# Queries, keys, gates and merge gates as 25 block-product pairs in one stage, and the dilated attention beside the branch products

## The chip, the cores and the metric

The kernel runs on one core of one Trainium2 chip. Five engines work side by side, each with an instruction queue that it executes in order: TensorE (PE in the profile, with its weight loads as PEld), VectorE (DVE), ScalarE (ACT), GpSimd (POOL) and SyncE (SP, which here issues most of the DMAs). They meet through semaphores. The metric is the time of one execution in microseconds (us), as the median of three runs. The profile shows one more execution, taken by the hardware profiler.

## The reference

One encoder block on 1024 tokens of width 1024 (`h` is the normalised input):

```python
h = rms_norm(x, g_pre)
a_qkv, bq, bk, bv, mq, ga, gb, gm, mg = split(h @ w_in)      # 1024 x 10496 in all
# A: 3 groups of 8 heads of 64, dilation 1, 4, 16, window of +-64 steps
aq, ak = rope(a_q, pos), rope(a_k, pos)
for g in groups: outs[g], lses[g] = dilated_window_attention(aq[g], ak[g], av[g])
oa = sum_g softmax_g(lses)[g] * outs[g]
# B: grouped-query attention with normalised queries and keys and axial rope; M: attention into 256 memory rows
ya = (oa * silu(ga)) @ w_br_a;  yb = (ob * silu(gb)) @ w_br_b;  ym = (om * silu(gm)) @ w_br_m
gates = sigmoid(mg + b_merge)                                 # 3 x 1024 columns: 24 units of 128
out = (gates[0]*ya + gates[1]*yb + gates[2]*ym) @ w_out
return x + rms_norm(out, g_post)
```

The projection `h @ w_in` is the largest part. Group A alone has 12 units of 128 columns for queries, 12 for keys and 12 for values; the SiLU gates have 12 units, the merge gates 24.

## The kernel before, in words

All operands are fp32. A matrix product is made from three passes: each operand is split by `split` (lines 104 to 106) into a rounded high part (ACT) and a remainder (DVE), and TensorE adds high x high, high x low and low x high. The tokens `h`, transposed, lie split in `hh[0..7]` and `hl[0..7]`, eight tiles of 128 x 1024 each.

There are two ways to make a unit, which is 128 columns of the projection for all 1024 tokens:

- *Plain* (`dense`, lines 139 to 147): 8 row blocks x 3 passes x 2 halves of 512 tokens = 48 matmuls with 512 columns. A unit can be cut anywhere, so `weave` (line 176) deals its matmuls out between the pieces of an attention: it compares the share of the filling that is done with the share of the attention that is done, by costs that the program gives each piece, and takes the one that is behind. Small jobs of the filling (evacuations, splits) stand in `pend` and are emitted one per three matmuls.
- *Pair* (Strassen's scheme in Winograd's form, `PRODUCTS`, line 896): two units by two token halves, each with two halves of the inner dimension, as seven block products instead of eight. A product has 4 row blocks x 3 passes = 12 matmuls, a pair 84. The sums of weight blocks (S1 to S4) are made on POOL, split by ACT and DVE, and the sums of token blocks (T1 to T4) are made once, kept in DRAM (`tsd`) and fetched and split where needed. Partial results are added on DVE as products leave PSUM.

The order of the stages, with the start of each in the profiled execution where the prediction speaks of it:

1. Norm, the keys and values of B, memory keys and values, queries of B and M, attention M; filling: plain gate units.
2. Attention B (`b_att`, from 218 us); filling (lines 868 to 877): five plain SiLU gate units and two plain merge gate units (`FILL_B`).
3. Values of A as block products (462 and 539 us).
4. Keys of A (579 us, lines 1251 to 1292): six pairs. Each result is multiplied by the rotation's cosine and sine tables (`turn_it`) and both products are stored to DRAM (`kd`).
5. Dilated attention (694 us, `item`, `plan`, lines 1399 to 1656): twelve items, one per head pair `p_` and group `g`, eight score tiles of 128 queries each. Per tile: scores (L1467, L1474, written into four PSUM banks `s1`, two tiles to a pair of banks), minimum with mask on DVE (L1486), exponential on ACT (L1487), transposes (L1498, L1513, L1522) three tiles later, a copy to SBUF on ACT (L1500, L1525), value products (L1539, L1546). `scores(1)` is emitted behind tile 3 and the next item's `scores(0)` behind tile 7, each behind value products. The filling is 16 plain units: the twelve query units of A, rotated in the same stage (DVE L1330, L1333, POOL L1334), and four SiLU gates (`GATES_A`). Keys come back from DRAM and are added on POOL (L1397).
   When the three groups of a head pair are done, `combine` (from L1658) weighs them: statistics are transposed and stored (L1572 to L1579), fetched (L1671), made into weights (L1676 to L1687), stored (L1692), fetched as broadcasts (L1666), multiplied in on DVE (L1701) and summed on POOL (L1703). The first three head pairs are combined in this stage, the last in the next.
6. Merge gates (982 us, lines 1714 to 1975): eleven pairs; sums of weights L1813, results to sigmoid form (DVE L1842, ACT L1843) and to DRAM (`thd`).
7. Branch products (1192 us, `y_unit`): 24 units of 24 matmuls, each attention output times its gate, split, times the branch weights; DVE multiplies each with its merge gate from `thd` (L2027, L2029) and POOL adds up (L2030).
8. Output product as block products and the last norm (1323 us).

From stage 3 on ACT, DVE, POOL and SP follow the order in which the program emits their work (`manual_schedule`), so what is emitted earlier on an engine runs earlier there, even when it has to wait.

Of the kernel before, what the change touches and what calls it, by code (L numbers as in the profile page):

```python
# [14 lines left out]
D = 1024  # L15
# [35 lines left out]
def block(ctx: ExitStack, tc: tile.TileContext, x, xT, memT, cst, msk, bcst, tabA, gpost,  # L51
# [5 lines left out]
    hp = ctx.enter_context(tc.tile_pool(name="hp", bufs=16))  # L57
# [78 lines left out]
    hh = [hp.tile([P, S], R, name=f"hh{k}", tag="big") for k in range(8)]  # L136
    hl = [hp.tile([P, S], R, name=f"hl{k}", tag="big") for k in range(8)]
# [73 lines left out]
    spilled = set()  # L211

    def add_filler(j):
        spilled.add(j)

        def evac(half, p):
            th = fp["p"].tile([P, 512], F32, name="fth", bufs=2)
            V.tensor_tensor(th, p, rb[:, half * 512:half * 512 + 512], op=OP.mult)
            A.activation(th, th, AF.Tanh, scale=0.5, bias=hbm[:, j:j + 1])
            nc.sync.dma_start(thd[j, :, half * 512:half * 512 + 512], th)  # L220
        add_unit(wu[U_M + j], evac)

# [17 lines left out]
    kd = dram.tile([2, 12, P, S], F32, name="kd")  # L240
# [471 lines left out]
    with tc.tile_pool(name="ba", bufs=1, reuse_waits="tile") as ba:  # L712
# [157 lines left out]
        for i in (2, 1, 0):  # L870
            for p_ in range(4):
                if (i, p_) not in ((2, 0), (2, 1), (2, 2)) + GATES_A:
                    add_gate(i, p_)
                    ng += 1
        for j in FILL_B:
            add_filler(j)
            ng += 1
# [20 lines left out]
    for k, t in enumerate(ready.pop(len(queue))):  # L898
        SB[0, k] = t
    vpp, vp = pool("vp")  # L900
# [24 lines left out]
    def parts_of(t):  # L925
        return t[:, lo], t[:, hi]
# [86 lines left out]
    def v_banks():  # L1013
# [5 lines left out]
    KT_PLACE = {"T2": ["kT20", "kT21", "kT22", "kT23"], "T3": ["vA220", "vA221", "kT32", "kT33"],  # L1019
                "T1": ["vA110", "vA111", "vA210", "vA211"], "T4": ["vS20", "vS21", "vA120", "vA121"]}  # L1020

    def kt_load(nm, k):
        KT[nm, k] = vb.tile([P, 1024], R, name=KT_PLACE[nm][k])
        nc.sync.dma_start(KT[nm, k][:, hi].bitcast(F32), tsd[int(nm[1]) - 1, k])
# [4 lines left out]

    KR = {}  # L1030

    def k_load(n, u):

        KR[n, u] = wp.tile([P, 1024], F32, name="wr", bufs=WR)
        nc.sync.dma_start(KR[n, u], wu[4 * n + 2 * u + 1])


    AU = [2 * m for m in range(12)] + [U_G + 4 * i + p_ for i, p_ in GATES_A]
    AR, AW = {}, {}

    def a_fetch(n):
        AR[n] = wp.tile([P, 1024], F32, name="wr", bufs=WR)
        nc.sync.dma_start(AR[n], wu[AU[n]])

# [1308 lines left out]
```

## Time and profile before

| | us |
|---|---|
| median of 3 runs | 1409.36 (1407.35 to 1410.84) |
| the profiled execution | 1409.89 |
| its span | 1408.1 |
| TensorE busy / DVE / ACT / POOL | 1384.0 / 1051.2 / 655.7 / 501.9 |
| keys, 579 to 694 | 115.1 |
| dilated attention, 694 to 982 | 287.8 |
| merge gates, 982 to 1192 | 210.1 |
| branch products, 1192 to 1323 | 131.1 |

An engine is busy while one of its instructions executes; TensorE's matmuls are pipelined, so the durations of neighbours overlap, and the spacing of their starts tells how fast they go. In a row of grouped instructions stand the line, the engine, the operation, output and input tiles, the shape and the count, then the busy time of the group, the mean duration of one in ns, and the idle time of the engine before them with what ended it. A row of the timeline starts with the start and the duration in us.

### The profile page before, as it was taken

To read this page: it belongs to the slowest core of one execution; us is meant where nothing else is said; L and a number is where in the kernel's file an instruction comes from. 1 tells how busy PE (TensorE), PEld (TensorE's weight loads), DVE (VectorE), ACT (ScalarE), POOL (GpSimd) and SP (SyncE) were. 2 spreads that over 40 slices of the span, in tenths; PEclk is the share of its full clock that TensorE was granted. 3 is DMA by queue.
4 is the path that set the end of the run, shared out by engine and by line. 5 is a ranking of instruction groups with operands and counts; after the bars stand their busy time and mean duration, and the time that the engine had idled before them with its cause. 6 is when DMAs were issued, how large, how long until landed. Compare 5 with 4: busy or idle time off the path is not lost.

```text
span 1408.1 us, 22008 instructions
## 1 busy us (share of the span) xinstructions
PE 1384.0 (98%) x7864; PEld 1120.3 (80%) x7864; DVE 1051.2 (75%) x1839; ACT 655.7 (47%) x1398; POOL 501.9 (36%) x390
## 2 busy tenths in 40 slices
PE   7999999999999999999999999999999999999997
PEld 7799986666656789988888878788888888888886
DVE  7768677767764697888775777765878688677977
ACT  6544465666555445222146666656443334222232
POOL 0507702675766000332153353621333331034303
PEclk9999999999999999999999999999999999999999
DMA  6356532322210788345544464455343543865255
GB/s 233 103 180 213 185 109 87 108 90 72 82 56 27 238 258 250 103 167 180 186 132 114 124 170 118 140 149 179 106 149 127 178 173 128 321 218 209 95 204 179
DMA packets 125950, 216.05 MB, mean 153 GB/s; under 512 B 33616, under 2 KB 62096, under 8 KB 125840
## 3 DMA queue, kind: packets, MB, share of 16 engines
q1 hardware_dynamic: 110192, 189.17, 42.0%
q10 hardware_dynamic: 15648, 25.47, 5.0%
q8 instruction: 62, 1.02, 0.3%
q14 instruction: 48, 0.39, 0.1%
HBM read 149.21 MB, written 65.37 MB: 152 GB/s over the span
## 4 chain that ended last, share of the span: by engine, by line
PE 86%; DVE 4%; ACT 4%; DMA 2%; POOL 2%; issue 2%; SPq 1%; DVEq 0%; ACTq 0%; POOLq 0%
PE s L125 24%; PE sc L125 9%; PE d L143 6%; PE d L147 6%; PE d L145 6%; PE s L1177 4%; PE s L2125 4%; PE ov L809 3%; PE s L1226 3%; PE s L794 2%; PE s L793 2%; PE tr L775 2%; PE d L2125 2%; PE s L1474 2%; PE tr L1546 1%
## 5 line engine op out<-in xcount | busy, mean ns | idle before, releaser
L143 PE MATMUL d<-hh,wh 128*128 128x512 f32 x480 | 194.3, 405 | 2.5 <-DVE fth L228 2.5
L145 PE MATMUL d<-hl,wh 128*128 128x512 f32 x480 | 193.4, 403 | 0.0
L147 PE MATMUL d<-hh,wl 128*128 128x512 f32 x480 | 190.3, 396 | 0.0
L800 POOL TENSOR_TENSOR bl<-bl,bp 128x512 f32<-128x512 f32 x96 | 130.8, 1363 | 54.4 <-ACT bp L796 49.0
L105 ACT ACTIVATE wh<-wr 128x512 fp32r<-128x512 f32 (+1 forms) x93 | 72.2, 787 | 124.5 <-PE sc L125 75.1
L106 DVE TENSOR_TENSOR wl<-wr,wh 128x1024 fp32r<-128x1024 f32 (+1 forms) x67 | 85.6, 1289 | 52.1 <-ACT wh L105 52.0
L125 PE MATMUL sc<-hh,wh 128*128 128x512 f32 x384 | 118.7, 390 | 0.0
L143 PEld LDWEIGHTS d<-hh,wh 128*128 128x128 f32 x480 | 90.3, 188 | 28.0 <-issue 5.5
L147 PEld LDWEIGHTS d<-hh,wl 128*128 128x128 f32 x480 | 90.5, 189 | 21.2 <-issue 4.7
L1487 ACT ACTIVATE pra<-pra,sts 128x192 f32<-128x192 f32 (+2 forms) x192 | 80.9, 423 | 54.3 <-DVE sts L1486 54.1
L145 PEld LDWEIGHTS d<-hl,wh 128*128 128x128 f32 x480 | 90.5, 189 | 19.5 <-issue 4.7
L796 ACT ACTIVATE bp<-s 128x512 f32<-128x512 f32 x128 | 75.7, 595 | 43.3 <-PE s L794 42.2
L776 DVE TENSOR_REDUCE bn<-tr 128x1 f32<-128x512 f32 x128 | 84.8, 683 | 12.3 <-PE tr L775 11.3
L125 PEld LDWEIGHTS sc<-hh,wh 128*128 128x128 f32 x384 | 72.0, 188 | 15.7 <-DVE wh L106 0.4
L1330 DVE SCALAR_TENSOR_TENSOR t2a<-d,tab 32x512 f32<-32x512 f32 x96 | 66.0, 687 | 22.0 <-PE d L147 18.6
L2030 POOL TENSOR_TENSOR acc<-acc,th 128x1024 f32<-128x1024 f32 x15 | 41.3, 2756 | 107.9 <-DVE th L2029 107.9
L1813 POOL TENSOR_TENSOR sf<-wr 128x512 f32<-128x512 f32 x22 | 30.8, 1422 | 131.4 <-DVE ch L106 45.7
L125 PE MATMUL sc<-hl,wh 128*128 128x512 f32 x192 | 74.7, 389 | 0.0
L125 PE MATMUL s<-hh,ch 128*128 128x512 f32 x224 | 73.7, 390 | 0.0
L1334 POOL TENSOR_TENSOR aq<-t1a,t2a 128x512 f32<-128x512 f32 x24 | 46.9, 1955 | 71.5 <-DVE t1a L1333 71.5
L1843 ACT ACTIVATE rs<-rs,hbm 128x512 f32<-128x512 f32 x44 | 31.8, 722 | 75.5 <-DVE rs L1842 75.5
L1397 POOL TENSOR_TENSOR ak<-kraw,kswp 128x512 f32<-128x512 f32 x24 | 45.9, 1939 | 51.7 <-DMA std<-sr 20.0
(507 smaller groups left out, 3748.7 us busy)
## 6 DMA issues: line engine op xcount, KB each, us to landing
wr<-in_wu SPq DMA_DIRECT2D x64, 512.0 KB
th<-thd SPq DMA_DIRECT2D x24, 512.0 KB
thd<-rs ACTq DMA_DIRECT2D x44, 256.0 KB
kd<-vy ACTq DMA_DIRECT2D x32, 256.0 KB
g2d<-fth SPq DMA_DIRECT2D x24, 256.0 KB
wos<-os SPq DMA_DIRECT2D x12, 512.0 KB
kraw<-kd SPq DMA_DIRECT2D x12, 512.0 KB
kswp<-kd SPq DMA_DIRECT2D x48, 128.0 KB
```

Source lines behind the costliest of these rows:

```text
L105: A.activation(dst_h, src, AF.Copy)
L106: V.tensor_tensor(dst_l, src, dst_h.bitcast(F32), op=OP.subtract)
L125: PE.matmul(out_ps, a, b, start=i == 0, stop=i == n - 1)
L143: PE.matmul(dst, wh[:, k, :], hh[k][:, t], start=k == 0, stop=False)
L145: PE.matmul(dst, wh[:, k, :], hl[k][:, t], start=False, stop=False)
L147: PE.matmul(dst, wl[:, k, :], hh[k][:, t], start=False, stop=k == 7)
L776: fp["last"] = V.tensor_reduce(st[i]["n"][:, j, c:c + 1], s, axis=AX.X, op=OP.min)
L796: A.activation(pp, s, AF.Exp, scale=-1.0)
L800: G.tensor_tensor(lsum[i % 2], lsum[i % 2], pp, op=OP.add)
L1330: V.scalar_tensor_tensor(t2[i], p[j], -0.125, tab[1][j, t], op0=OP.mult, op1=OP.mult)
L1487: A.activation(src, src, AF.Exp, scale=-1.0, bias=bias, accum_out=sts[:, h, 1, T:T + 1])
L2125: PE.matmul(dst[:, e[0]:e[1]], a, b, start=k == 0 and q == 0, stop=k == 3 and q == 2)
```

## The change

- Keys and merge gates, until now two stages of pairs, become one stage of 25 pairs: twelve pairs that make the queries and the keys (`("rope", m)`), one pair of SiLU gates (`GATES_P`) and twelve of merge gates, in alternation (`PAIRS`). Queries are no longer plain units. Two SiLU gates more take the place of the two merge gates beside attention B.
- Products that end in the same sum accumulate in one PSUM bank (`skip_group_check`); ACT copies the intermediate values out (`keep_copy`) where DVE added before. The next pair's first product stands between a pair's own.
- The weights' columns are laid out so that the two units of a query or key pair hold the first and the second half of each head's rotation. `c_fin` multiplies by the tables (DVE), `turn_it` adds (POOL), in the order of the group's classes, and `k_store` writes finished queries and keys to `qkd`.
- The dilated attention stands behind that stage. Its filling is the first 16 of the 24 branch units, in the order memory, B, A (`add_y`); the last eight, branch A, follow. Operands of the memory branch are loaded, multiplied and split in the last pair (`op_load`, `op_mult`, `op_split`). `y_split` makes the remainders of branch weights on POOL there; transposed probabilities are copied on DVE instead of ACT; weighting of the first three head pairs moves from DVE to POOL. The last head pair is combined at the end of this stage (`ending`).
- Sums, evacuations and the output stage keep their arithmetic; some tiles get other places.

```diff
-    for n in range(6):
-        for i, (an, bn) in enumerate(PRODUCTS):
...
+    TURNS = [(j, c, g) for c in range(2) for g in range(3) for j in (1, 0)]
+    pairs = [(8 * i + f, 8 * i + f + 1) for i in (2, 1, 0) for f in range(0, 8, 2)]
+    others = [("gate", 0)] + [("merge", m) for m in range(12)]
+    PAIRS = [x for m in range(12) for x in (("rope", m), others[m])] + [others[12]]
...
+    def c_fin(n, u, t, ps_=None):
+        r = kr() if ps_ is not None else RV.pop((n, u, t))
+        src = r if ps_ is None else ps_
+        kind, m = PAIRS[n]
+        if kind != "rope":
+            V.tensor_tensor(r, src, rb[:, half[t]], op=OP.mult)
...
+                A.activation(r, r, AF.Tanh, scale=0.5, bias=hbm[:, j:j + 1])
+                nc.scalar.dma_start(thd[j, :, half[t]], r)
+            return
...
+    def turn_it(n, t):
...
+        G.tensor_tensor(half_of(o1, t, g), classes(ac, g), classes(bs, g), op=OP.subtract)
+        G.tensor_tensor(half_of(o2, t, g), classes(as_, g), classes(bc, g), op=OP.add)
...
+    def op_load(t):
+        for k in range(4):
+            if k % 2 == 0:
+                OPM[t, k // 2] = vb.tile([P, 1024], F32, name=f"vA12{k // 2}")
+            for dst, src in ((OPM[t, k // 2], od), (tab[k // 2], g2d)):
+                nc.sync.dma_start(dst[:, half[k % 2]], src[2, k, :, t])
...
+    def y_split(m, E=V):
+        if m < len(steps):
+            t = wp.tile([P, 1024], R, name="wh")
+            A.activation(t[:, lo], YW[m][:, lo], AF.Copy)
+            E.tensor_tensor(t[:, hi], YW[m][:, lo], t[:, lo].bitcast(F32), op=OP.subtract)
...
+    def th_load(m):
...
+            THS[m] = wp.tile([P, S], F32, name="wl")
+            nc.sync.dma_start(THS[m], thd[8 * i + f])
+
+    def y_evac(m, t, ps_):
...
+            V.scalar_tensor_tensor(th[:, t], th[:, t], 1.0, ps_, op0=OP.add, op1=OP.mult)
+            (V if m == 23 else G).tensor_tensor(accs[f][:, t], accs[f][:, t], th[:, t], op=OP.add)
...
+    pair_product(0, "A11")
+    pair_product(0, "A12")
+    keep_copy(p1, 0)
+    for n in range(last + 1):
+        N = n + 1
+        pair_product(n, "S2")
+        c_add(*((n - 1, 0, 1, BANK[n - 1, "W"], v_) if n else (0, 0, 0, BANK[0, "Y"], p1)))
+        k_block(n, "A22")
...
+        pair_product(n, "S1")
+        keep_copy(v_, n)
...
+            op_split(lo, 2)
+            op_split(lo, 3)
+            qk_first(0)
+            y_load(0)
+            op_load(hi)
+            y_load(1)
+            qk_first(1)
+        pair_product(n, "S3")
+        k_block(n, "S4")
...
+        pair_product(*((N, "A11") if n < last else (n, "S4")))
+        keep_copy(y_, n)
...
+        pair_product(n, "A22")
...
+        pair_product(N, "A12")
+        c_fin(n, 1, 0, BANK[n, "X"])
+        k_block(N, "S2")
...
+        pair_product(n, "S4")
...
-                A.activation(pp[:, :k], tp[:, :k], AF.Copy)
+                V.tensor_copy(pp[:, :k], tp[:, :k])
...
-                V.tensor_tensor(ogv, ogv, wv, op=OP.mult)
+                (G if p_ < 3 else V).tensor_tensor(ogv, ogv, wv, op=OP.mult)
                 if g:
                     G.tensor_tensor(ogs[0], ogs[0], ogs[g], op=OP.add)
...
+        def add_y(m):
+            n, i, f = steps[m]
+            def gen(_):
+                pend.extend([lambda: th_load(m + 1), lambda: y_load(m + 2), lambda: y_split(m + 1, G)])
+                for t in half:
+                    ps_ = psd()
+                    wh, wl = YW[m]
+                    for k in range(4):
+                        gh, gl = [x[k][:, t] for x in OPER[i]]
+                        for q, (a, b) in enumerate(((wh[:, k], gh), (wh[:, k], gl), (wl[:, k], gh))):
+                            PE.matmul(ps_, a, b, start=k == 0 and q == 0, stop=k == 3 and q == 2)
+                            yield 216
+                    pend.append(lambda t=t, ps_=ps_: y_evac(m, t, ps_))
+            queue.append((lambda: None, gen, 24 * 216.0))
...
+        def ending():
+            com = combine(3, [OG.pop((3, x)) for x in range(3)])
+            return [(com[0], 100.0), (out_pool, 100.0), (lambda: dl_mult(2), 100.0), (lambda: dl_split(2, half), 6000.0),
+                    (com[1], 3000.0), (com[2], 100.0), (lambda: [wo_load("B11", k) for k in range(2)], 100.0),
+                    (com[3], 4000.0), (lambda: [wo_load("B11", k) for k in range(2, 4)], 100.0),
+                    (com[4], 5000.0), (com[5], 100.0), (com[6], 100.0), (com[7], 100.0),
...
+                    (lambda: dl_mult(3), 3000.0), (lambda: dl_split(3, half), 3000.0)] + [
+                    (lambda k=k: wo_split("B11", k), 1500.0) for k in range(4)]
...
+        weave(16, every(), FIRST_PAD + 12 * (NT * (SOFT + 100.0) + 2 * JOINED + 100.0) + 5 * LAST_PAD + 33000.0)
...
-FILL_B = (16, 17)
-GATES_A = ((0, 0), (0, 1), (0, 2), (0, 3))
+FIRST_PAD, LAST_PAD = 7000.0, 1000.0
+GATES_P = ((0, 2), (0, 3))
```

More of the change, by code (lines that the diff above doesn't have):

```diff
@@ L1294, in block @@
+    c_fin(last, 1, 0, BANK[last, "X"])
+    for k in range(4):
+        op_split(hi, k)
+    r = RV[last, 0, 1]
+    V.tensor_tensor(r, BANK[last, "Z"], r, op=OP.add)
+    c_fin(last, 0, 1)
+    c_fin(last, 1, 1)
     close(kpp)
+    close(tbp)
     close(vbp)
```

751 lines of the change are left out of this document (273 added, 478 removed).

## The prediction

> **What bounds the kernel now.** The first view is the page's busy shares.
>
> ```profile
> span 1408.1 us, 22008 instructions
> PE 1384.0 (98%) x7864; PEld 1120.3 (80%) x7864; DVE 1051.2 (75%) x1839; ACT 655.7 (47%) x1398; POOL 501.9 (36%) x390
> ```
>
> TensorE has a matmul in flight for 98% of the span; the others are far below. A busy share is only a hint, so I read the stages next: the chain of waits, which gives their borders, and then the busy time of each engine in each stretch (columns: PE, weight loads, DVE, ACT, POOL, granted clock, DMA share, GB/s).
>
> ```profile
> 579.34 115.13 PE s L125 x504
> 982.23 207.36 PE s L125 x912
> 1189.59 2.72 PE d L125 x12
> 1192.31 131.08 PE sc L125 x576
> ```
>
> ```profile
> 462.08:539.27 77.19, 77.19 (x339) 63.19 (x338) 61.63 (x98) 35.24 (x59) 0.00 (x0) 1.00 0.83 265
> 579.34:694.47 115.13, 115.13 (x505) 94.73 (x505) 96.55 (x125) 27.62 (x46) 34.03 (x21) 1.00 0.48 159
> 694.47:982.23 287.76, 284.90 (x2389) 232.72 (x2388) 204.22 (x598) 166.60 (x546) 107.71 (x55) 1.00 0.53 147
> 982.23:1192.31 210.08, 210.08 (x925) 173.47 (x926) 169.00 (x214) 89.28 (x138) 72.38 (x45) 1.00 0.42 141
> 1192.31:1323.39 131.08, 131.08 (x577) 107.95 (x577) 97.38 (x84) 34.70 (x55) 41.35 (x15) 1.00 0.63 223
> ```
>
> Keys (579 to 694), merge gates (982 to 1192) and branch products (1192 to 1323) run without any gap on TensorE: 504, 924 and 576 matmuls of 512 columns at 228.4, 227.4 and 227.6 ns each. I take 227.7 ns. The dilated attention (694 to 982) has 2.9 us of gaps. Its filling is these three groups, restricted to that stretch:
>
> ```profile
> L143 PE MATMUL d<-hh,wh 128*128 128x512 f32 x256 | 104.9, 410 | 0.0
> L145 PE MATMUL d<-hl,wh 128*128 128x512 f32 x256 | 104.5, 408 | 0.0
> L147 PE MATMUL d<-hh,wl 128*128 128x512 f32 x256 | 100.9, 394 | 0.0
> ```
>
> 768 matmuls, or 174.9 us; so the attention's own matmuls and transposes take 284.9 - 174.9 = 110.0 us of TensorE, and the filling covers everything else. So TensorE's issue time is the bound, and what matters is the number of matmuls and whether TensorE is ever left with nothing.
>
> **The change, part by part.** *Number of matmuls.* A plain unit of 128 columns costs 48 matmuls, a block-product pair (two units) 84. Before: 30 plain units and 17 pairs. After: 14 plain units (7 remain beside the axial attention, as before, two of them now gates instead of merge gates) and 25 pairs. 16 x 48 = 768 go and 8 x 84 = 672 come: 96 fewer, 21.9 us.
>
> *By stage.* Pairs: 25 x 84 = 2100 x 0.2277 = 478.2. Attention: its own 110.0 plus 16 branch units of 24 matmuls, 384 x 0.2277 = 87.4. The eight branch units behind it: 192 x 0.2277 = 43.7. Together 719.4, against 115.13 + 287.76 + 210.08 + 131.08 = 744.0 before. Everything else stays (218.0 and 244.1 to 462, 117.3 for the values, 84.7 at the end). Without any new wait the span would be 1408.1 - 24.6 = 1383.5. What is left is the price of thinner cover: filling per score tile falls from 48/8 to 23/8 matmuls, about 6 to 3.
>
> *Pair stage: costed at nothing.* Per pair DVE does one split of 1024 and thirteen to fourteen operations of 512 (five splits, three sums from PSUM, some six rotations or gate products), 14 x 0.69 + 1.3 = 11.0 us of the pair's 19.1. The key stage did it with 96.55/6 = 16.1 us of DVE per pair and lost nothing. POOL gets the rotation's sums, ACT the tanhs; neither fills a pair. The 96 stores of rotated rows and 50 weight loads queue on SP but are needed a pair or more later. The bounds are 0 and the price of the third rival; I take 0, as the key stage's row is the nearest.
>
> *Entry to the attention.* The first branch unit needs od[2] x gate split into hh and hl, and half of it overwrites tokens that the last product reads. On SP that load stands behind the first queries and keys and a weight: 2 x 0.524 + 0.262 + 8 x 0.262 = 3.4 MB, startable when product S2 of the last pair has let go of its tokens, 2.7 us into the pair. At the 265 GB/s of the values stage (a rate under load, so an estimate) that is 12.9 us, to 15.6. Then come the second gate product, a last merge gate's product and tanh, and four splits one after another.
>
> ```profile
> L1881 DVE SCALAR_TENSOR_TENSOR ot<-ot,raw 128x1024 f32<-128x1024 f32 x2 | 2.4, 1222 | 0.0
> L106 DVE TENSOR_TENSOR wh<-wr,wh 128x512 fp32r<-128x512 f32 x23 | 15.7, 685 | 1.8 <-ACT wh L105 1.8
> L1843 ACT ACTIVATE rs<-rs,hbm 128x512 f32<-128x512 f32 x2 | 1.4, 724 | 2.8 <-DVE rs L1842 2.8
> ```
>
> 15.6 + 1.2 + 0.7 + 0.7 + 0.6 + 4 x 0.7 = 21.6, where TensorE, after 60 matmuls of the shortened last pair (13.7) and 12 + 9 of the first unit (4.8), wants the fourth split at 18.5. That is a wait of 3 us, and 1 more as ACT copies a bank behind two splits in that pair: 4 (0 if the load comes early, 8 if the product waits for the whole).
>
> *Within the attention.* Some 23 filling matmuls per item keep TensorE supplied if DVE and ACT finish in time. DVE loses the rotation and gains ACT's 80 copies of transposed probabilities and 32 branch evacuations:
>
> ```profile
> L1330 DVE SCALAR_TENSOR_TENSOR t2a<-d,tab 32x512 f32<-32x512 f32 x96 | 66.0, 687 | 22.0 <-PE d L147 18.6 <-POOL aq L1334 1.7
> L1487 ACT ACTIVATE pra<-pra,sts 128x192 f32<-128x192 f32 (+2 forms) x192 | 80.9, 423 | 54.3 <-DVE sts L1486 54.1
> L1525 ACT ACTIVATE app<-tr 128x384 f32<-128x384 f32 (+1 forms) x64 | 33.5, 523 | 26.3 <-PE tr L1522 16.3 <-PE tr L1513 9.5
> ```
>
> 66.0 goes from DVE, 80 x 0.52 = 42 of copies (at ACT's price) and 32 x 0.69 = 22 of evacuations come, which is even; but the weight splits and nine weighted products of 2.0 go to POOL, so DVE's 204 us falls to about 160 in a stage of about 212, and ACT's 167 to about 130. Neither is the bound on average. POOL gets sixteen splits of branch weights, those products and sixteen sums; the split for unit 6 stands behind two products and sums of the first head pair, about 6 us, with fifteen filling matmuls and half an item, some 8 us, as cover: nothing, and each microsecond by which POOL is later is TensorE's. Twelve items at a quarter microsecond each make 3 us. Before lost 2.9 (lower bound 0); the upper bound is the second rival.
>
> *End of the attention.* The last head pair's combination stood beside eleven merge pairs; now branch units 16 to 23 need its result. The chain, from an earlier head pair (SP, DVE, POOL):
>
> ```profile
> 843.05 3.10 SPq L1579 DMA_DIRECT2D std<-sr  x3
> 848.05 1.30 SPq L1671 DMA_DIRECT2D cpt<-std  x2
> 858.94 1.25 SPq L1692 DMA_DIRECT2D wgd<-ceg  x2
> 860.84 3.71 SPq L1666 DMA_DIRECT2D wgt<-wgd  x6
> ```
>
> ```profile
> 856.70 0.17 DVE L1676 TENSOR_TENSOR cmn<-cpt 128x16 f32<-128x16 f32 x1
> 858.70 0.21 DVE L1687 TENSOR_TENSOR ceg<-ceg,cds 128x48 f32<-128x48 f32 x1
> 865.83 2.00 DVE L1701 TENSOR_TENSOR og<-og,wgt 128x1024 f32<-128x1024 f32 x1 [1.04 <-DMA wgt<-wgd]
> 868.10 1.96 DVE L1701 TENSOR_TENSOR og<-og,wgt 128x1024 f32<-128x1024 f32 x1 [0.27 <-DMA wgt<-wgd]
> 870.20 2.39 POOL L1703 TENSOR_TENSOR og<-og 128x1024 f32<-128x1024 f32 x1 [4.33 <-DVE og L1701]
> ```
>
> Statistics to SBUF 0.7, four stores and landing 3.0 (846.15 to 848.05 bounds the landing by 1.9), fetch and landing 3.2, weights 2.2, store to the start of the first product 6.9 (858.94 to 865.83), then three products paced by their loads to about 6.5 later, the last POOL sum 2.4, gate product 1.2, first split 1.3: 27.4 us. In the built order 79 branch matmuls follow that last transpose of statistics (18.0 us), with the last value products (1.1) and nine matmuls of unit 16 (2.0): 21.1. In two queues more is waiting. On SP the weight loads stand behind a load of thd that waits for POOL's sum of unit 13; by my count that frees as the chain arrives. On POOL the split of unit 16's weights stands behind the last sums, and TensorE wants it at the unit's third matmul, 1.5 us sooner. So TensorE waits 27.4 + 1 - 21.1 + 1.5 = 8.8, of which I take 8.5; between 3, if loads land faster, and 13.
>
> Sum: 1383.5 + 4 + 3 + 8.5 = 1399.0. The profiled execution took 1409.89 for a span of 1408.1, so 1.8 lies outside it, and it stood 0.5 above the median of 1409.36: 1399.0 + 1.8 - 0.5 = 1400.3, 0.6% faster. A measurement here can tell about 0.3%, 4.2 us.
>
> **Rivals.** *Covers are thicker than I think*: entry and end cost 0 and 3 and items nothing. 1383.5 + 3 + 1.3 = 1388; I round to 1390.
>
> *Slower: the hand-over of score banks.* The third and fourth score tiles of a half item go to banks that the softmax of the third and fourth before must have read; after the value products TensorE waits there.
>
> ```profile
> 856.43 0.35 DVE L1486 CUSTOM_DVE_ANT_0 pra<-s,mask 128x192 f32<-128x192 f32 x1
> 856.01 1.48 PE L1546 MATMUL tr<-app,avs 128*64 128x128 f32 x24
> 857.42 1.81 PE L1474 MATMUL s<-ak,aq 64*128 64x128 f32 x24
> ```
>
> DVE was done at 856.8, the second half of the scores ran from about 858.3: 1.5 us in hand. Three filling matmuls fewer per tile bring TensorE there up to 4 x 3 x 0.228 = 2.7 us earlier, so up to 1.2 may be missing at each of 23 hand-overs: 28 us, 1383.5 + 12.5 + 28 + 1.3 = 1425. Against it: DVE was held up by rotations that are gone. It turns the change into a loss from 0.5 us per hand-over.
>
> *DVE and POOL hamper each other in the pair stage.*
>
> ```profile
> 878.45 4.31 POOL L1397 TENSOR_TENSOR ak<-kraw,kswp 128x512 f32<-128x512 f32 x2 [5.85 <-DMA std<-sr]
> 878.85 2.76 DVE L1701 TENSOR_TENSOR og<-og,wgt 128x1024 f32<-128x1024 f32 x1
> ```
>
> With POOL at work the product that took 2.00 takes 2.76, 1.38 times. At that ratio a pair's DVE work is 11.0 x 1.38 = 15.2 us, still under 19.1; at 1.8 times 19.8, and the 25 pairs lose 17 us: 1418. The Trainium skill (GPSIMD Engine Reference, Specifications) says that POOL shares its SBUF interfaces with the vector engine when the latter reads two SBUF inputs; the two durations of the product agree.
>
> *TensorE's clock falls in the new waits.* At the start the same matmul was spaced twice as far for some 3 us:
>
> ```profile
> 8.22 0.41 PE L381 MATMUL s<-wbh,hh 128*128 128x256 f32 x1
> 8.43 0.41 PE L381 MATMUL s<-wbh,hl 128*128 128x256 f32 x1
> 14.28 0.28 PE L381 MATMUL ov<-wbh,hh 128*128 128x256 f32 x1
> 14.39 0.28 PE L381 MATMUL ov<-wbh,hl 128*128 128x256 f32 x1
> ```
>
> If entry and end each bring that again, 3.2 us at half pace lose 1.6, twice, and together with a whole microsecond more per item 1400.3 + 3.2 + 5 = 1408.5: no difference. The Trainium skill (TensorE: Matmul & The Clock Gate, Part 1) has a rule for it: an idle window of about 3.4 us halves the clock until a busy one has passed; by it alone the sum would be 1403.5. No wait before was that long, and the granted clock was 1.00 in each row above, so no row decides it.
>
> **Chances.** Forecast, 1391 to 1405: 0.48; thicker covers: 0.12; clock and small waits, no difference: 0.16; hand-over: 0.16; DVE against POOL: 0.08. Faster 0.60, same 0.16, slower 0.24. The range leaves out the best end and the worst of the hand-over: 1391 to 1422.
>
> **What would show it.** The pair stage 2100 matmuls in 478 us without gaps; the attention 197 us of TensorE in about 212; a gap of some 4 us at the first branch unit's second half and of 6 to 9 before unit 16, ended by DVE or POOL; score matmuls without waits. I am wrong if gaps stand before L1529's second halves, if DVE is full in the pairs, or if the end chain is twice as long.

## The result and the profile after

The changed kernel takes 1469.04 us (median of four runs, 1467.70 to 1472.26) against 1409.51 in the same comparison: 1.0427 times, 95% interval 1.0406 to 1.0449. It is 4.3% slower, 69 us above the forecast of 1400.3 and outside its range. The profiled execution has a span of 1466.9, which answers to 1399.0 in the forecast's sum.

The page of the changed kernel, first part and row of the granted clock:

```profile
span 1466.9 us, 21800 instructions
PE 1388.7 (95%) x7768; PEld 1109.3 (76%) x7768; DVE 1028.3 (70%) x1797; ACT 659.9 (45%) x1378; POOL 600.4 (41%) x455
PEclk9999999999999999999999999999999999888999
```

96 matmuls are gone (7864 to 7768), as counted. But TensorE is no longer in flight for 98% of the span, and late in it the clock is not full. The rows below show the stages: the pairs; the entry and the items of the attention up to the transpose of its last statistics; from there to unit 16; the branch tail; the output. The columns are as in the prediction: the stretch, its length, busy time of TensorE, weight loads, DVE, ACT and POOL, the granted clock, the DMA share and GB/s.

```profile
578.78:1082.62 503.84, 489.73 (x2101) 394.37 (x2101) 353.71 (x385) 175.44 (x278) 244.82 (x145) 1.00 0.36 111
1082.62:1300.00 217.38, 188.62 (x1890) 148.98 (x1889) 125.15 (x528) 125.99 (x447) 67.78 (x36) 0.95 0.62 190
1300.00:1338.10 38.10, 23.83 (x116) 18.17 (x116) 20.58 (x26) 5.75 (x12) 19.70 (x13) 0.79 0.58 169
1338.10:1381.90 43.80, 43.63 (x191) 35.83 (x192) 43.52 (x37) 15.50 (x29) 22.81 (x9) 1.00 0.56 190
1381.90:1466.90 85.00, 77.19 (x349) 63.48 (x347) 66.87 (x107) 26.37 (x61) 13.21 (x22) 0.98 0.49 174
```

Tail and output are as forecast (43.8 and 85.0 against 43.7 and 84.7). The pairs take 503.8 instead of 478.2: **25.6 over**. Up to the last statistics the attention's own work (without the last value products, 1.1) and 305 filling matmuls are 110.0 - 1.1 + 305 x 0.2277 = 178.3, and the stretch takes 217.4: **39.1 over**, where 4 + 3 were forecast. From there 79 filling matmuls, the last value products and unit 16's first two matmuls are 19.5 of 38.1: **18.6 over**, where 8.5 was forecast. Together this is 83.3, against the 15.5 allowed for; the difference is the miss.

In the attention, these groups carry most of the waits (grouped by line, window from the last pair to unit 16; after the bar stand busy time, mean ns of one, and the idle time before them with what ended it):

```profile
L1815 PE MATMUL d<-bh,wh 128*128 128x512 f32 x128 | 49.2, 444 | 17.9 <-DVE wl L1344 17.9
L1815 PE MATMUL d<-hh,wh 128*128 128x512 f32 x128 | 46.3, 417 | 2.7 <-ACT hh L105 2.5 <-ACT wh L1326 0.2
L1529 PE MATMUL s<-ak,aq 64*128 64x128 f32 (+2 forms) x336 | 31.1, 325 | 0.6 <-DVE vy L1427 0.6
L1601 PE MATMUL tr<-app,avs 128*64 128x128 f32 x352 | 30.5, 296 | 5.6 <-DVE app L1580 5.5
L1614 PE MATMUL tr<-cs,sts 128*32 128x128 f32 x12 | 3.5, 294 | 6.5 <-DVE app L1580 6.0 <-ACT og L1609 0.4
```

TensorE mostly waits for DVE: for banks of the filling (L1815, emptied by L1344) and for copies of probabilities (L1580). The score matmuls (L1529) hardly wait. The filling's mean is 417 to 444 ns where it was 394 to 410 before.

**Pair stage.** One group has nearly all its waits, eight of 1.4 to 1.6 us; one more, of 2.0, stands in the last pair. This is one of the eight in the timelines of TensorE, ACT, DVE and POOL:

```profile
L1292 PE MATMUL s<-hh,vS 128*128 128x512 f32 x400 | 134.6, 398 | 12.1 <-ACT vrt L1296 12.1
```

```profile
691.90 0.39 PE L1292 MATMUL s<-hh,wl 128*128 128x512 f32 x1
693.87 0.50 PE L1292 MATMUL s<-hh,vS 128*128 128x512 f32 x1 [1.58 <-ACT vrt L1296]
...
692.09 0.72 ACT L1106 ACTIVATE vv<-vv,hbm 128x512 f32<-128x512 f32 x1 [5.09 <-DVE vv L1098]
692.85 0.33 ACTq L1107 DMA_DIRECT2D thd<-vv  x1
693.22 0.60 ACT L1296 ACTIVATE vrt<-s 128x512 f32<-128x512 f32 x1 [0.40 <-ACT vv L1106]
...
679.16 2.53 DVE L106 TENSOR_TENSOR vS<-vot,vS 128x512 fp32r<-128x512 f32 x1
681.62 2.63 DVE L106 TENSOR_TENSOR vS<-vgt,vS 128x512 fp32r<-128x512 f32 x1
690.77 0.68 DVE L106 TENSOR_TENSOR vS<-vot,vS 128x512 fp32r<-128x512 f32 x1
691.38 0.68 DVE L1098 TENSOR_TENSOR vv<-vv,rb 128x512 f32<-128x512 f32 x1
...
679.01 2.13 POOL L1127 TENSOR_TENSOR ko<-wl,vy 128x512 f32<-128x512 f32 x1
681.10 2.60 POOL L1128 TENSOR_TENSOR ko<-wh,vv 128x512 f32<-128x512 f32 x1
```

ACT is idle for 5.1 us in front of a merge gate's tanh, whose input DVE makes late; the copy that frees the bank for the next product stands behind that tanh in ACT's order. DVE is late because two splits took 2.53 and 2.63 beside POOL's rotation sums, where the one at 690.77, with POOL idle, took 0.68.

**Within the items.** DVE stands in front of a gate product whose loads SP issued only just before. Copies and evacuations that TensorE needs stand behind it (DVE, SP, TensorE):

```profile
1277.39 1.23 DVE L1798 SCALAR_TENSOR_TENSOR aq<-aq,ak 128x1024 f32<-128x1024 f32 x1 [8.90 <-issue]
1278.53 0.55 DVE L1580 COPY app<-tr 128x384 f32<-128x384 f32 x1
1295.24 1.23 DVE L1798 SCALAR_TENSOR_TENSOR aq<-aq,ak 128x1024 f32<-128x1024 f32 x1 [5.71 <-DMA ak<-g2d]
1296.39 0.68 DVE L1344 SCALAR_TENSOR_TENSOR wl<-wl,d 128x512 f32<-128x512 f32 x1
...
1272.24 0.55 SPq L1794 DMA_DIRECT2D aq<-od  x1
...
1279.14 0.40 PE L1614 MATMUL tr<-cs,sts 128*32 128x128 f32 x1 [6.03 <-DVE app L1580]
1297.12 0.80 PE L1815 MATMUL d<-bh,wh 128*128 128x512 f32 x1 [3.80 <-DVE wl L1344]
```

**End chain** (SP, DVE, TensorE):

```profile
1300.76 1.30 SPq L1634 DMA_DIRECT2D std<-sr  x4
1302.99 1.27 SPq L1730 DMA_DIRECT2D cpt<-std  x2
1312.40 1.27 SPq L1751 DMA_DIRECT2D wgd<-ceg  x2
1314.88 1.66 SPq L1334 DMA_DIRECT2D wl<-thd  x1
1317.12 3.99 SPq L1725 DMA_DIRECT2D wgt<-wgd  x6
...
1310.30 0.16 DVE L1735 TENSOR_TENSOR cmn<-cpt 128x16 f32<-128x16 f32 x1
1323.75 1.91 DVE L1760 TENSOR_TENSOR og<-og,wgt 128x1024 f32<-128x1024 f32 x1 [10.13 <-DMA wgt<-wgd]
1328.49 3.60 DVE L1760 TENSOR_TENSOR og<-og,wgt 128x1024 f32<-128x1024 f32 x1 [0.57 <-DMA wgt<-wgd]
1332.01 0.68 DVE L1344 SCALAR_TENSOR_TENSOR wl<-wl,d 128x512 f32<-128x512 f32 x1
1334.64 2.29 DVE L1798 SCALAR_TENSOR_TENSOR og<-og,ak 128x1024 f32<-128x1024 f32 x1 [1.95 <-POOL og L1762]
...
1300.04 0.40 PE L1614 MATMUL tr<-cs,sts 128*32 128x128 f32 x1 [0.42 <-ACT og L1609]
1332.75 0.80 PE L1815 MATMUL d<-bh,wh 128*128 128x512 f32 x1 [13.88 <-DVE wl L1344]
```

From the transpose of the last statistics (1300.04) to the end of the last gate product (1336.9) it is 37 us. TensorE stands 13.9 of them in unit 15, whose bank waits for an evacuation (L1344) behind the three products.

### The profile page after: what moved, and what is told of

Same layout as the page of the kernel before. It is cut to its first block, busy times and chain, and to the rows that moved or that the text cites. A ratio compares the mean times of both kernels' runs of the same rounds, so it can differ in the third digit from the quotient of the medians.

```text
span 1466.9 us, 21800 instructions
## 1 busy us (share of the span) xinstructions
PE 1388.7 (95%) x7768; PEld 1109.3 (76%) x7768; DVE 1028.3 (70%) x1797; ACT 659.9 (45%) x1378; POOL 600.4 (41%) x455
## 4 chain that ended last, share of the span: by engine, by line
PE 70%; DVE 11%; issue 6%; ACT 4%; DMA 4%; POOL 3%; SPq 1%; ACTq 0%; DVEq 0%; POOLq 0%
PE s L1292 24%; PE s L1204 4%; PE s L1968 4%; PE ov L797 3%; PE sc L125 3%; PE s L1253 3%; PE d L145 3%; PE d L147 3%; PE d L143 3%; DVE vS L106 3%; PE s L782 2%; PE s L781 2%; PE tr L763 2%; PE d L1815 2%; PE tr L1601 2%
## 5 line engine op out<-in xcount | busy, mean ns | idle before, releaser
L1292 PE MATMUL s<-hh,vS 128*128 128x512 f32 x400 | 134.6, 398 | 12.1 <-ACT vrt L1296 12.1
L1292 PE MATMUL s<-vA,vS 128*128 128x512 f32 x450 | 109.6, 394 | 2.0 <-ACT vv L1296 2.0
L1292 PEld LDWEIGHTS s<-vA,vS 128*128 128x128 f32 x450 | 83.6, 188 | 23.8 <-ACT vv L1296 6.1
L143 PE MATMUL d<-hh,wh 128*128 128x512 f32 x224 | 89.3, 399 | 2.4 <-DVE fth L216 2.4
L147 PE MATMUL d<-hh,wl 128*128 128x512 f32 x224 | 89.4, 399 | 0.0
L145 PE MATMUL d<-hl,wh 128*128 128x512 f32 x224 | 88.8, 397 | 0.0
L1292 PE MATMUL s<-hl,vS 128*128 128x512 f32 x200 | 79.0, 395 | 0.0
L1292 PE MATMUL s<-hh,wl 128*128 128x512 f32 x200 | 78.2, 391 | 0.0
L1292 PE MATMUL s<-hh,wh 128*128 128x512 f32 x200 | 78.2, 391 | 0.0
L1292 PE MATMUL s<-hl,wh 128*128 128x512 f32 x200 | 77.8, 389 | 0.0
L1815 PE MATMUL d<-bh,wh 128*128 128x512 f32 x128 | 49.2, 444 | 17.9 <-DVE wl L1344 17.9
L1580 DVE COPY app<-tr 128x384 f32<-128x384 f32 (+1 forms) x64 | 38.7, 605 | 38.5 <-PE tr L1568 23.6
```

The costliest lines, as they stand in the source:

```text
L143: PE.matmul(dst, wh[:, k, :], hh[k][:, t], start=k == 0, stop=False)
L145: PE.matmul(dst, wh[:, k, :], hl[k][:, t], start=False, stop=False)
L147: PE.matmul(dst, wl[:, k, :], hh[k][:, t], start=False, stop=k == 7)
L1292: PE.matmul(BANK[n, c], a, b, start=k == 0 and q == 0 and not more, stop=k == 3 and q == 2, skip_group_check=c in "XW")
L1815: PE.matmul(ps_, a, b, start=k == 0 and q == 0, stop=k == 3 and q == 2)
```

## The experiments

Each experiment starts from the changed kernel (1469.04 us). These theories were to be told apart: **C**, the attention's chains have too little TensorE work beside them; **O** and **S**, the pair stage's waits come from ACT's order (O) or from POOL stretching DVE (S); **D** and **Q**, DVE stands in front of loads (D) or splits (Q) and holds the copies behind; **E**, the last head pair's chain lies bare; **W**, the waits halve the clock. Times are medians; the ratio is to the kernel before in the same comparison (the changed kernel itself: 1.0427).

| run | us | ratio, 95% interval |
|---|---|---|
| a1_turn_dve | 1461.16 | 1.0365 [1.0349, 1.0380] |
| a2_double_fill | 1505.76 | 1.0683 [1.0665, 1.0701] |
| a3_no_last_combine | 1452.77 | 1.0308 [1.0292, 1.0323] |
| a4_late_products | 1468.25 | 1.0413 [1.0398, 1.0429] |
| b1_copies_act | 1463.88 | 1.0391 [1.0375, 1.0406] |
| b2_k3_last | 1469.81 | 1.0442 [1.0421, 1.0463] |
| b3_copy_first | 1455.85 | 1.0336 [1.0319, 1.0353] |
| b4_warm | 1472.93 | 1.0454 [1.0435, 1.0472] |
| c1_mended | 1454.85 | 1.0324 [1.0309, 1.0339] |
| c2_mended_act | 1444.84 | 1.0251 [1.0234, 1.0268] |
| c3_mended_act_hold | 1453.52 | 1.0316 [1.0301, 1.0332] |
| c4_gates_early | 1444.91 | 1.0247 [1.0230, 1.0265] |
| c5_gates_early_dve | 1442.19 | 1.0234 [1.0219, 1.0250] |

**Double filling.**

```diff
-PE.matmul(ps_, a, b, start=k == 0 and q == 0, stop=k == 3 and q == 2)
+PE.matmul(ps_, a, b, start=k == 0 and q == 0, stop=False)
+PE.matmul(ps_, a, b, start=False, stop=k == 3 and q == 2)
 yield 216
```

> Each of the 384 branch matmuls that fill the attention is issued twice; the second adds the same product again, so these branch products come out doubled. 384 matmuls of 0.2277 us are 87.4 us of more work on TensorE. Theory C (the attention loses its 58 us because the cover beside it is too thin, and the end chain lies bare): the added work goes into the waits, the stage takes about 110 + 175 + 8 = 293 us instead of 255.7, the time is 1469 + 37 = 1506, the granted clock in it 1.00. Rival (TensorE is held up by blocked queues whatever its cover): the added work comes on top, 1469 + 87 = 1556, with the waits as they were.

Measured: 1505.76, 36.7 more for 87.4 us more of work. The stage's row (last pair to unit 16):

```profile
1082.60:1372.70 290.10, 285.83 (x2388) 232.92 (x2387) 150.37 (x554) 135.00 (x460) 90.42 (x49) 0.99 0.55 166
```

With 768 filling matmuls, as before the change, the attention has 4 us of waits and a clock of 0.99, with the same orders on all queues and the same loads. So theory C holds: beside the 384 filling matmuls some 50 us of TensorE's time lie idle or at half clock. The run does not say which links of the chains are the long ones.

**The pair stage: POOL's sums to DVE, and the copy before the tanh.**

```diff
-G.tensor_tensor(half_of(o1, t, g), classes(ac, g), classes(bs, g), op=OP.subtract)
-G.tensor_tensor(half_of(o2, t, g), classes(as_, g), classes(bc, g), op=OP.add)
+V.tensor_tensor(half_of(o1, t, g), classes(ac, g), classes(bs, g), op=OP.subtract)
+V.tensor_tensor(half_of(o2, t, g), classes(as_, g), classes(bc, g), op=OP.add)
```

> The sums of the rotation move from POOL to DVE; nothing else changes. Theory S (POOL at work stretches DVE's operations on two SBUF inputs, from 0.68 to as much as 2.5 us; so the tanh behind them comes late on ACT, and the copy of a bank behind that tanh holds TensorE eight times for 1.6 to 1.7 us in the pair stage): the eight waits go, DVE's splits in the pairs fall back to about 0.7 us, the pair stage (503.8 us to its last product) shortens by 13 to 18 us, the time is 1469 - 15 = 1454. Rival (the order on ACT alone does it, or DVE is then too full, since 48 sums of 0.7 us come to it): no gain, 1466 to 1475, the waits still there.

```diff
-        c_fin(n, 0, 0)
         pair_product(*((N, "A11") if n < last else (n, "S4")))
         keep_copy(y_, n)
+        c_fin(n, 0, 0)
```

> In the pair stage the last quarter of a pair's evacuation (with its tanh) is put behind the copy of the next product's bank, so that ACT does the copy first. DVE and POOL do what they did. Theory O (order on ACT: the copy stands behind a tanh whose input DVE has not made yet): the eight waits of 1.5 us go as well as with the sums moved off POOL, pair stage 504.0 to about 492, 1469 - 11 = 1458. Rival (the stretched DVE work is needed by TensorE anyway, in its splits): waits of the same size in other places, 1466 to 1470.

Measured: 7.9 us faster, which lies between theory S and its rival, and 13.2 us faster. First comes the pair stage of the first run; then the pair stage of the second and its attention; then one split in the pair stage (grouped by line and shape) in the changed kernel, in the first run and in the second:

```profile
578.56:1071.97 493.41, 489.14 (x2103) 394.78 (x2102) 363.10 (x433) 176.33 (x279) 158.39 (x97) 1.00 0.36 114
```

```profile
578.50:1068.20 489.70, 487.71 (x2103) 395.37 (x2102) 353.45 (x385) 176.72 (x279) 245.16 (x145) 1.00 0.36 114
1068.20:1322.90 254.70, 214.44 (x2004) 169.42 (x2004) 144.79 (x551) 130.46 (x456) 86.46 (x48) 0.91 0.61 187
```

```profile
L106 DVE TENSOR_TENSOR vS<-vgt,vS 128x512 fp32r<-128x512 f32 x24 | 37.2, 1549 | 0.0
```

```profile
L106 DVE TENSOR_TENSOR vS<-vgt,vS 128x512 fp32r<-128x512 f32 x25 | 18.1, 726 | 0.0
```

```profile
L106 DVE TENSOR_TENSOR vS<-vgt,vS 128x512 fp32r<-128x512 f32 x25 | 37.8, 1513 | 0.0
```

With the sums on DVE the split takes 726 ns instead of 1549: POOL did stretch it. The eight waits shrink from 12.1 us to six that make 2.2, and the stage falls by 10.4 us to 493.4; in the profiled execution some 4 us were lost again in the attention (259.4 against 255.5), for a reason that no run shows. With the copy first the eight waits go altogether although the split stays at 1513, and the stage falls by 14.1 us to 489.7. The stretched work makes the tanh late; only the order on ACT makes TensorE pay. The last run, which has both, fits this (below).

**The last head pair's chain left out.**

```diff
 com = combine(3, [OG.pop((3, x)) for x in range(3)])
+com = [lambda: None] * 7 + [com[7]]
```

> Leaves out the combination of the last head pair: no fetch of its statistics, no weights, no products, no sums; its first branch alone goes on to the gate. Theory E (the wait of 13.9 us in unit 15 and the half clock after it come from this chain alone, 40 us long instead of 27.4): unit 16 starts when the filling is used up, about 1322 instead of 1337 in the span, the time is 1469 - 15 = 1454. Rival (other things late at the same place hold it: the split of unit 16's weights on POOL, the gate products on DVE, the loads on SP): 1462 to 1469.

Measured: 16.3 us faster. From the last statistics to unit 16 (TensorE busy throughout):

```profile
1301.40:1322.20 20.80, 20.80 (x114) 16.71 (x115) 11.86 (x16) 7.65 (x14) 15.95 (x11) 0.94 0.63 219
```

20.8 us against 38.1 with the chain: 17.3 of the 18.6 us lost at the end are this chain, as theory E said.

**Gate products later; copies on ACT.**

```diff
-elif (n, T) in ((10, 7), (11, 6)):
-    dl_mult(n - 10)
-elif (n, T) in ((11, 1), (11, 7)):
-    dl_split(T // 7)
+elif (n, T) == (11, 1):
+    dl_mult(0)
+    dl_split(0)
```

(The product and split of head 1 follow the fetch of the last statistics.)

> The first two gate products of the output branch (heads 0 and 1) are put later in DVE's order, each behind about half an item after its load instead of right behind it; nothing is left out. Theory D (DVE stands 8.9 and 5.7 us in front of these products waiting for their loads, and what is queued behind, the copies of probabilities and the evacuations of branch banks, stops TensorE for 6.0 and 3.8 us and halves its clock): both waits go, with about 3 us of half clock, the time is 1469 - 11 = 1458. Rival (the end chain sets the end, and what is gained before it is lost again in its wait): 1466 to 1469 with the waits gone.

Measured: 0.8 us, no difference. The waits did not go: DVE still stood 5.7 us in front of the first product, and TensorE 6.5 at the item's value products. So this run alone does not test theory D; the first kernel with all mends (below) does. The last statistics came 4.6 us earlier (1295.40) and unit 15 then waited 16.2 instead of 13.9: what was gained was lost again at the end, as the rival said.

```diff
-V.tensor_copy(pp[:, :k], tp[:, :k])
+A.activation(pp[:, :k], tp[:, :k], AF.Copy)
```

(The same edit stands at the other copy of probabilities.)

> The 80 copies of transposed probabilities in the attention go back from DVE to ACT. Theory Q (they come late because DVE, which works in order, stands in front of them in splits and products whose input is not there): the waits of TensorE that DVE's copies end, 17 us in all, go for the greater part, ACT's 143 us of work in the attention become 185; the end chain keeps its length, so some 5 to 10 us are left: 1461. Rival (ACT stands as long in front of its half of the same splits, and every exp is now behind the copies): the waits only change their name, 1466 to 1472.

Measured: 5.2 us faster. The waits on DVE's copies went, but 10.5 us of waits on ACT's copies stand before the transposes instead (grouped by line, window 1082 to 1340):

```profile
L1568 PE MATMUL tr<-cs,pra 128*128 128x128 f32 x120 | 21.9, 292 | 15.4 <-ACT app L1580 10.5 <-ACT sr L1621 2.8 <-ACT og L1609 1.7
```

The time lies at the near end of theory Q. For more than half of the 17 us of waits the rival's words hold: they changed their name. The last statistics came 5.9 us earlier (1294.1), and this gain was kept to the end.

**Work in the waits.** Units 16 and 17 with head 3 last:

```diff
+    AHEAD = {16: pss(), 17: pss()}
+    y_part(16, AHEAD[16], range(3))
+    y_split(17)
+    y_part(17, AHEAD[17], range(3))
     for m in range(16, 24):
...
+        if m in AHEAD:
+            s = AHEAD[m]
+            y_part(m, s, (3,))
...
```

(`y_part` issues a unit's products with the heads named; the filling's evacuations also stand before the last three products.)

> Units 16 and 17 issue the products with heads 0 to 2 (18 matmuls each, 8.2 us together) before those with head 3, and the evacuations of the filling units are put ahead of the last head pair's three products on DVE. Theory E (the end chain has a fixed length, and TensorE waits only because nothing independent is left beside it): the chain ends where it did, 8.2 us of work move into its wait and some half clock goes: 1469 - 9 = 1460. Rival (the chain itself moves with what is put beside it, or unit 16's weights are late): 1466 to 1469.

Measured: no gain. Only unit 16's 18 matmuls went into the wait; unit 17's weights were split on ACT at 1340.1, behind the last gate's splits and four weight splits of the output stage, and TensorE waited 11.9 us for them. So the run leaves theory E's question open here, and shows one more wait that comes from order.

Useless matmuls in unit 15's wait:

```diff
...
+if m == 15 and t is half[1]:
+    spare = pst().rearrange("p a b -> p (a b)")
+    for r in range(56):
+        PE.matmul(spare, wh[:, 0], OPER[i][0][0][:, t], start=r == 0, stop=r == 55)
...
```

> 56 matmuls of 512 columns whose result nobody reads (12.8 us at 0.228) are put into unit 15, just where TensorE waits 13.9 us for its bank. Theory W (that wait halves the clock, and the end is set by the chain beside it): the added work costs nothing, the 13.7 us of half clock there go down to 3.4 or none, the twelve matmuls behind it and unit 16 run at 0.23 us each, 1 to 2 us are gained: 1467 to 1469. Rival (TensorE's work at that place counts): up to 1469 + 13 = 1482.

```profile
1319.00:1336.20 17.20, 17.20 (x76) 13.94 (x75) 7.19 (x5) 0.63 (x1) 7.26 (x3) 1.00 0.74 229
```

The 12.8 us of matmuls cost 3.9 by the medians, with overlapping intervals, and 1.0 between the two spans. So most of them went into the wait, as theory W had it, and the clock there is 1.00 instead of 0.50. But nothing is gained, against the theory: unit 16 then waits 2.1 us for its weights on POOL.

**Together.** All mends of order in one kernel: the copy first, gate products of heads 0 to 2 behind the last item, evacuations before the last products, unit 17's weights before them, units 16 and 17 with head 3 last.

```diff
...
+            return [(com[0], 100.0), (out_pool, 100.0), (lambda: dl_mult(0), 100.0), (lambda: dl_split(0, half), 100.0),
+                    (lambda: dl_mult(1), 2000.0), (lambda: dl_split(1, half), 100.0),
+                    (com[1], 6900.0), (com[2], 100.0),
+                    (com[3], 100.0), (lambda: [dl_gate(2, "q"), dl_gate(3, "k")], 100.0),
+                    (lambda: [wo_load("B11", k) for k in range(4)], 100.0),
+                    (lambda: dl_mult(2), 5000.0), (lambda: dl_split(2, half), 100.0),
+                    (flush, 1e6), (com[4], 100.0), (com[5], 100.0), (com[6], 100.0), (com[7], 100.0),
...
```

> The copy of the bank before the tanh in the pair stage; the gate products of heads 0 to 2 behind the last item and behind the last head pair's weights; its three products behind the evacuations of the filling; unit 17's weights split before them; units 16 and 17 with head 3 last. If the three losses found so far (order on ACT in the pairs 14 us; DVE in front of loads 10 us; 8 us of uncovered chain) are separate and add up: 1469 - 14 - 10 - 8 = 1437. If whatever is gained before the last statistics is lost again in the chain's wait, only the pairs' part is left: 1469 - 14 = 1455.

The second has the copies of probabilities on ACT as well:

> As the one before, with the copies of probabilities on ACT. They alone gave 5 us; where DVE's waits in front of loads are gone already, the part of these 5 us that came from them is gone too: 0 to 5 us faster than the kernel before it, 1432 to 1437 by the first theory.

The third keeps some of the filling back for the end:

```diff
-        weave(16, every(), FIRST_PAD + 12 * (NT * (SOFT + 100.0) + 2 * JOINED + 100.0) + 5 * LAST_PAD + 33000.0)
+        weave(16, every(), FIRST_PAD + 12 * (NT * (SOFT + 100.0) + 2 * JOINED + 100.0) + 5 * LAST_PAD + 51000.0)
```

> As the second, with about 80 of the 384 filling matmuls kept back from the items for the time behind the last statistics. If TensorE's time is lost for want of filling all over (the attention has 197 us of work for a stage set by its chains), it is a zero-sum: what the chain gains the items lose, within 3 us of the kernel before it. If only the end is bare, 8 to 15 us faster.

Measured: the first takes 1454.85, the pairs' part alone, as the second reading said. The last statistics came at 1275.8 instead of 1300.0, 14 us of it from the pairs and 10 from the items, but those 10 were lost again in the end chain. With the copies on ACT the second takes 1444.84, 10 us better where 0 to 5 were expected, a miss: the last statistics came 9 us earlier than in the first, and this gain was kept. What decides whether a gain in the items is kept to the end or lost there stays open. The third kept back 31 matmuls, not 80 (274 instead of 305 come before the last statistics), and was 8.7 us slower than the second, which neither theory had. The items were no shorter without these 7 us of work (last statistics at 1268.7 against 1266.7), and at the end they came on top: they stand behind the same bank, whose evacuation waits on DVE behind a gate product (TensorE 11.4 us, in the second kernel 12.4). So taking filling from the items shortened nothing there, which fits items whose length their chains set.

In two more, against the second of these, the loads of two gates come earlier, and then the rotation's sums go to DVE as well:

```diff
                     (lambda: dl_mult(1), 2000.0), (lambda: dl_split(1, half), 100.0),
+                    (lambda: [dl_gate(2, "q"), dl_gate(3, "k")], 100.0),
                     (com[1], 6900.0), (com[2], 100.0),
-                    (com[3], 100.0), (lambda: [dl_gate(2, "q"), dl_gate(3, "k")], 100.0),
+                    (com[3], 100.0),
```

> As the second mended kernel, with the loads of the gates of heads 2 and 3 issued before the last head pair's weights are stored and fetched, not behind. Theory B (each loss at the end is DVE standing in order in front of a load, here 11.7 us for a gate, with the evacuations that TensorE needs behind it): that wait and TensorE's 12.4 us go, the chain ends some 10 to 15 us earlier: 1445 - 12 = 1433. Rival (the chain through the last weights, 40 us from the last statistics, sets the end in any order): 1442 to 1446.

> As the one before, with the rotation's sums on DVE as well. If the copy's place behind the tanh was the whole of the pair stage's eight waits, the stretched DVE work no longer costs anything: no difference, within 2 us of the kernel before it. If stretched DVE work still holds TensorE in smaller pieces (the pair stage is 489.6 us for 478), some 4 to 8 us faster.

Measured: 1444.91, nothing gained, as the rival said, though the wait aimed at is gone. Behind it stood the next (DVE, then TensorE):

```profile
1300.59 1.28 DVE L1344 SCALAR_TENSOR_TENSOR wl<-wl,d 128x512 f32<-128x512 f32 x2 [11.21 <-DMA wl<-thd]
...
1318.47 0.79 PE L1907 MATMUL sc<-hh,wh 128*128 128x512 f32 x1 [5.14 <-ACT hh L105]
```

The last three products now stood behind an evacuation waiting for its merge gate's load, TensorE stood 9.5 us for unit 16's weights, which were loaded late, and the way from the last statistics (1268.5) to head 3 (1318.5) was 50 us. The rotation's sums on DVE as well made 2.7 us, with overlapping intervals: with the copy first, POOL's stretching costs these 2.7 us at most. The best kernel is still 2.3% slower than the one before the change.

## Why the prediction was wrong

*Count and stages without waits: right.* 96 matmuls went; the tail took 43.8 (43.7 forecast), the output 85.0 (84.7).

*Pair stage, "costed at nothing": wrong by 25.6 us.* The step compared DVE's work per pair (11.0) with the pair's length and never asked in which order ACT holds its operations. DVE was not full: 353.7/25 = 14.1 us of 20.2. 14 of the 25.6 are the copy behind the tanh (shown by the copy put first). About 11.5 remain with these waits gone (489.7 against 478.2), and the trace of that run divides them. Of the 2100 spacings between matmul starts, 2069 average 0.2304 us instead of 0.2277, which makes 5.5 us; the wait in the last pair costs 2.2, the half clock behind it 1.6, and twenty spacings of about 0.3 us make 2 more. So the term 2100 x 0.2277 itself was small by some 1%; why the spacing is wider here than in the merge gates before (0.2274) stays open.

*The rival that DVE and POOL hamper each other (0.08, 1418): half right.* Its sign and, by chance, its price (17) were near, and the stretch was larger than the 1.38 taken from one row. But it needed a full DVE; what happened was a late tanh in front of a copy. The Trainium skill (GPSIMD Engine Reference, Specifications) names two SBUF inputs of a DVE instruction as one case in which POOL and DVE contend. The trace agrees: the splits, with two, were stretched, and the additions that read a bank (L1090) kept 0.684 us.

*Entry, 4 us: right in the main.* There is one wait of 2.5, ended by ACT's split, and two below 0.6. The microsecond more for a bank copy of ACT in the last pair was 2.0 and stands in the pairs' row.

*Within the attention, 3 us: the step that failed most.* Without the entry's 3.3 the items lost 39.1 - 3.3 = 35.8. "Neither is the bound on average" was true (DVE 125.2, ACT 126.0 of 217.4) and said nothing of the delays: each tile is a chain through TensorE, DVE, ACT, TensorE and DVE, and the filling has to last as long as this chain, together with whatever stands ahead of its links in order (a split, a gate product, a load). Doubling the filling removed nearly all of the waits. By the time from the first filling matmul to the last statistics, some 10 us went with DVE's gate products moved (first kernel with all mends) and 8 more with the copies on ACT (second); the other 17 were not divided further. That 23 matmuls per item would do where 48 had done was carried over from a stage that had 48.

*The rival of the score banks (0.16, 1425)* had about the right size, 28 us in the items, and the wrong place: its score matmuls waited 0.6 us. TensorE waited for copies and evacuations.

*The clock (0.16, 1408.5): mechanism right, size far too small.* 37.5 us of the attention, in five stretches, ran at a granted clock of 0.50. An estimate from the intervals between its matmuls puts the cost at 12 to 14 us, where 3.2 was allowed for two waits. The rival's sum has a slip as well: a whole microsecond more for each of twelve items is 12 us, not 5, which gives 1415.5.

*End chain, 8.5 us: right mechanism, too short.* It was to be 27.4 against 21.1 of cover. Three links were mis-sized. Fetch to weights took 7.3 (1302.99 to 1310.30) instead of 3.2, since on DVE the splits of another head stood in front. The prediction's own rows had 8.6 between these two points (848.05 to 856.70); it priced the transfer and not the queue. Store to first product took 11.4 (1312.40 to 1323.75) instead of 6.9: on SP two loads of output weights, a merge gate's load that took 1.7 us to issue and a branch weight stood in front, which is 2.8 of the 4.5 more, and the broadcasts came later after their issue, which is the rest. The last product took 3.60 where 2.0 was forecast, and the gate product 2.29 instead of 1.2. The evacuation behind the three products, which stopped TensorE in unit 15 already, was not seen. "The end chain is twice as long" was named as what would make the forecast wrong; to the end of the gate product it took 36.9 instead of 26.1, two fifths more.

## What to carry to other kernels

Filling is not worth only its matmuls: beside latency chains it is also what covers them, so a change that shortens the filling should be priced by the chain per tile, order of queues included, and not by busy shares. Here 16 units of plain products cost 175 us and covered 288; without half of that work the stage shortened by 32 us, and not by 87. An operation that frees a bank for TensorE belongs ahead of anything on its engine that waits for another engine.

## What the runs showed of the hardware

The clock fell without long waits. Stretches of half clock start and end on a grid of 3.41 us in the trace of every changed kernel. These are four of the grid's windows in the changed kernel:

```profile
1070.20:1073.60 3.40, 1.39 (x6) 0.99 (x6) 1.89 (x3) 1.98 (x5) 0.00 (x0) 1.00 0.27 98
1073.60:1077.00 3.40, 3.40 (x10) 2.62 (x9) 1.81 (x3) 2.19 (x4) 0.00 (x0) 0.50 0.67 159
1083.80:1087.20 3.40, 1.54 (x7) 0.94 (x5) 1.83 (x2) 0.75 (x2) 0.95 (x1) 1.00 1.03 417
1087.20:1090.60 3.40, 2.35 (x8) 1.34 (x8) 2.76 (x5) 2.17 (x4) 0.00 (x0) 1.00 0.94 333
```

A window with a matmul in flight for 1.39 us of 3.40 was followed by one at half clock, one with 1.54 was not. From 1000 to 1420 us in the traces of all the kernels, full-clock windows with TensorE in flight for less than 0.43 of their time were always followed by half clock, those between 0.43 and 0.54 went either way, none above 0.54 was followed by it, and full clock came back only behind a window of 0.78 or more. "In flight" is the profile's modelled time. So a wait of 2 us, like the one in the last pair (its window is the first row), can halve the clock if it falls into one window. The Trainium skill (TensorE: Matmul & The Clock Gate, Part 1) has the window of 3.413 us and speaks of an idle window. The trace agrees on the grid, but here the window need not be idle as a whole.

DVE splits of 128x512, which read two SBUF inputs, took up to 3.9 times as long beside POOL's rotation sums (0.68 to 2.63 us), where the prediction's row, for a product, had 1.38.
